# A hybrid attention and DeltaNet layer: one scan record per chunk, key and query chunks loaded by step, projections in another order

## Chip, core and metric

One core of a Trainium2 chip runs the whole program; it has one instruction stream for each engine (TensorE = PE, VectorE = DVE, ScalarE = ACT, GpSimd = POOL, SyncE = SP, which only issues DMAs). The metric is device time in microseconds (us), less is better.

## What is computed

Two layers; each normalises the tokens (256 context, 1024 sample), projects them once, runs latent attention and a two-way gated DeltaNet beside each other, gates both, projects them out and adds the residual.

```python
h = rmsnorm(x, norm_w) * (1.0 + scale) + shift
z = jnp.einsum('bsd,de->bse', h, w_in)
q_lat, kv_lat, k_pe, g_a, q_b, k_b, v_b, g_b, a_b, b_b = jnp.split(z, offs, axis=-1)
...
o_a = mla_attention(q_nope, q_pe, kv[..., :NOPE], kpe_all, kv[..., NOPE:]) * jax.nn.silu(g_a)
...
o_f, s_f = chunk_gated_delta(qc, kc, vc, g[:, :, 0], beta[:, :, 0], s0[:, 0])
o_r, s_r = chunk_gated_delta(flip(qc), flip(kc), flip(vc), flip(g[:, :, 1]), flip(beta[:, :, 1]), s0[:, 1])
...
out = jnp.einsum('bse,ed->bsd', jnp.concatenate([o_a, o_b], axis=-1), w_out)
x = x + gate * out
```

In the delta rule each chunk solves a triangular system, and a state of 128x128 is carried from chunk to chunk, once forward and once backward.

## The kernel before

The 1280 tokens are ten chunks of 128. The projection is 24 tiles of 128 columns (`misc`, `l0`, `l1`, `lk` of the latent attention, `k`, `q`, `v` of four DeltaNet heads, gates `ga`, `gb`); a tile is three products in split precision over eight blocks of the model dimension, `zp` in the trace. The string `ORDER` says in which order `w_thread` makes them. Their weights come by DMA (`wr`) and are split by DVE and POOL (`wh`, `wl`).

A DeltaNet head h goes through four pieces of code, each a Python generator ("thread"):

- `gram_thread` loads the head's keys and queries (`kq`) from the DRAM tensor `kqv_d`, in which the convolved projections lie, transposes the keys (`ktp`), makes for each chunk the products k·k and q·k (`gram`), scales them with decays (`dm`, `ai`) and writes them to DRAM, to `ai_d`. `kp_thread` makes on POOL the keys for the state update (`kpt`) and writes them to `kp_d`. `q_thread` takes the norm of the queries.
- `inv_thread` inverts the 32x32 diagonal blocks of all chunks at once: 31 pairs of DVE instructions (`wtmp`, then `W`), each waiting for the one before. Then, by `ph` and `px` on PE, the blocks are put together to the inverse of each chunk, which goes back into `ai_d`.
- `g_thread` is the scan: four chains (two directions, sample and context tokens), eight steps. A step loads its record `ti` (inverse and q·k) and `kp`, and is a line of dependent work: `ks` on PE (keys times state), `ru` on DVE, `up` on PE, a copy on ACT, `su` on PE, the state `S` on DVE, and `po` for the output. Keys and queries of the step are read from `kq`, which stays in SBUF as long as the scan runs. Since `kq` has two buffers, `gram_thread(h)` waits for the flag `scan{h-2}`.

The attention starts when all projections are done: `rope`, then for each of eight heads `prep` (`kp`, `qp` and the row maxima `pm`, each reduced by DVE, ending in one transposition `mxt`) and `main` (scores `sp`, exponentials on ACT, `po`). `main` of a head waits for its `prep`. After that comes the output projection, `wop`. DeltaNet heads that are not done run beside the attention.

The order of instructions on each engine is fixed when the program is built. Every engine call passes a helper (line 312) and is queued with its thread; a planner (`Sched.run`) takes again and again the call that can start first by its table of costs and latencies, with the thread's number in `PR` to break ties. Where the planner sees PE without work for too long it puts in filler matmuls whose result nobody reads (`spare`, line 433). Buffers of a pool are named by tag, with `bufs` copies each.

Of the kernel before, what the change touches and what calls it, by code (L numbers as in the profile page):

```python
# [16 lines left out]
P = 128  # L17
# [10 lines left out]
HB = 4  # L28
# [8 lines left out]
TAIL = 6  # L37
ORDER = 'misc k0 q0 v0 l0 l1 gb0 lk ga0 k1 q1 v1 k2 q2 v2 k3 q3 v3 gb1 gb2 gb3 ga1 ga2 ga3'
PR = dict(ada=2.2, w=2.5, e=2.4, load=2.3, s=1, g=2, p=2.1, kp=2.2, q2=2.2, lat=1, oa=2.45, rope=2.44, prep0=3, prep=3, vv=3, main=4, fin=2, ex=4, red=3, red0=3, prec=5, ldc=4.5, mm=5, fc=1)
# [355 lines left out]
def body(tc, I, O):  # L395
# [163 lines left out]
    def mixer(l, hhl):  # L559
# [6 lines left out]
        ap = bp = None  # L566
        kp_d = [dp.tile([NT, 2, P, P], F32, name=f"kp_d{l}_{h}") for h in range(HB)]
        ai_d = [dp.tile([2, NT, 2 * P * P + P], F32, name=f"ai_d{l}_{h}") for h in range(HB)]
        fl = lambda t: t.rearrange("p a b c -> p (a b c)")
# [305 lines left out]
        def w_thread():  # L875
            order = ORDER.split()
            need = {'q0': 'misc2', 'lk': 'latq', 'k1': 'latk'}
            steps = [(nm, (0, 1, 2)) for nm in order[:-TAIL]]
# [144 lines left out]
        def gram_thread(h):  # L1023
            if h:
                yield f"A{h-1}"
            if h >= 2:
                yield f"scan{h-2}"
            yield f"k{h}"
# [3 lines left out]
            be, gc, grow_d, kdx = (st_[q] for q in ("be", "gc", "grow_d", "kdx"))  # L1032
            kq = ap.tile([P, 2, TP], F32, tag="kq", name="kq", bufs=2)
            SY.dma_start(kq[:, 0, :], kqv_d[h][0])
# [26 lines left out]
            V.tensor_scalar(n2, k2, EPS, None, op0=ALU.add)  # L1061
            nn = ap.tile([P, NT], F32, tag="nn", name="nn", bufs=3)
            G.tensor_tensor(nn, n2, pw[:, 1:2].to_broadcast([P, NT]), op=ALU.pow)
# [3 lines left out]
            for d in range(2):  # L1067
                V.tensor_tensor(bp[:, d], be[:, d, :, h], n2, op=ALU.mult)
                V.tensor_tensor(kdb[:, d], kdx[:, d, :, h], bp[:, d], op=ALU.mult)
            hd[h] = dict(kq=kq, nn=nn)  # L1070
            sd.flag(f"nn{h}")
# [7 lines left out]
            for c in range(NT + 1):  # L1079
# [13 lines left out]
                if pend:  # L1093
                    x, px, pdm, pbk = pend
                    ai = ap.tile([P, 2, 2, P], F32, tag="ai", name="ai", bufs=2)
                    for d in range(2):
                        V.scalar_tensor_tensor(ai[:, d], in0=px, scalar=bp[:, d, x : x + 1], in1=pdm[d].unsqueeze(1).to_broadcast([P, 2, P]), op0=ALU.mult, op1=ALU.mult)
                    free(pbk)
                    SY.dma_start(ai_d[h][:, x, : 2 * P * P].rearrange("d (p a q) -> p d a q", p=P, a=2), ai)
                pend = (c, pt, dms, bk)  # L1100
# [3 lines left out]
        def inv_thread(h):  # L1104
# [24 lines left out]
            for d in range(2):  # L1129
                SY.dma_start(diag(wz, d), (WP if d else W)[64 * d : 64 * d + 40])  # L1130
                SY.dma_start(diag(ai_d[h], d), (W if d else WP)[64 * d : 64 * d + 40])
            for c0, m in groups:
                yield 0
# [39 lines left out]
        def kp_thread(h, ktok, kdb):  # L1173
            for c in range(NT):
                t = ap.tile([P, 2, P], F32, tag="kpt", name="kpt", bufs=2)
                for d in range(2):
                    G.tensor_scalar(t[:, d], ktok[:, c, :], kdb[:, d, c : c + 1], None, op0=ALU.mult)
                SY.dma_start(kp_d[h][c].rearrange("d p q -> p d q"), t)
                yield 0
            sd.flag(f"kp{h}")  # L1180

        def q_thread(h, kq):
            q2 = ap.tile([P, NT], F32, tag="q2", name="q2", bufs=3)
            for c0, m in groups:
# [13 lines left out]
        def g_thread(h):  # L1198
# [3 lines left out]
            yield f"nn{h}"  # L1202
            nn, kq = hd[h]["nn"], hd[h]["kq"]
            neg_eg, pos_eg, gle = (st_[q] for q in ("neg_eg", "pos_eg", "gle"))
            kch = lambda c: kq[:, 0, coff(c) : coff(c) + P]
            qch = lambda c: kq[:, 1, coff(c) : coff(c) + P]
            vt = ap.tile([P, TP], F32, tag="oT", name="vt", bufs=1)
# [29 lines left out]
            def load_rec(n):  # L1237
                for ci, d, c, samp, last in steps(n):
                    ti = ap.tile([P, 2, P], F32, tag="ti", name="ti", bufs=6)
                    SY.dma_start(ti, ai_d[h][d, c, : 2 * P * P].rearrange("(p a q) -> p a q", p=P, a=2))  # L1240
                    kp = None
                    if not (samp and last):
                        kp = ap.tile([P, P], F32, tag="kp", name="kp", bufs=6)
                        SY.dma_start(kp, kp_d[h][c, d])
                    rec[ci, n] = (ti, kp)

            load_rec(0)
            load_rec(1)
            for n in range(8):
# [6 lines left out]
                for ci, d, c, samp, last in act:  # L1256
                    if not (samp and last):
                        kps[ci] = rec[ci, n][1]
                    if state[ci] is not None:
                        p1s[ci] = yield from bank("ks")  # L1260
                        PE.matmul(p1s[ci][:, :P], kch(c), state[ci])
                yield 0
# [35 lines left out]
                for ci, d, c, samp, last in act:  # L1298
# [3 lines left out]
                    if old[ci] is not None:  # L1302
                        PE.matmul(po[:, 1, :], qch(c), old[ci])
                    pos[ci] = (po, bk)
# [509 lines left out]
        for h in range(HB):  # L1814
            sd.add(PR['p'], gram_thread(h))
            sd.add(PR['p'], inv_thread(h))
            sd.add(PR['g'], g_thread(h))
        sd.run()
# [87 lines left out]
```

## Time and profile before

| | |
|---|---|
| median of 3 runs | 2248.81 us (2247.12 to 2254.36) |
| the profiled execution | 2256.47 us |
| its span, first to last instruction | 2254.7 us |
| busy: PE, DVE, ACT, POOL | 2132.3, 1484.5, 772.3, 824.1 us |
| mean granted TensorE clock | 0.982 |
| DMA: moved, mean rate | 306.91 MB, 136 GB/s |

A busy time is the union of an engine's instructions. The granted clock is given as a share of full speed: 1.0 is 2.4 GHz, the lower level is 1.2 GHz, and a mean between them says how long each was granted. The DMA share is the mean busy share of the core's 16 DMA engines. A view of windows gives all of these for stretches counted in us from the span's start.

### The profile page before, as it was taken

The page shows a single profiled execution, that of the slowest core. Times are in us where ns is not written, and L with a number is a line of the kernel's source. Part 1 is how long each engine was busy: PE and PEld are TensorE (multiplying, and loading weights), DVE is VectorE, ACT ScalarE, POOL GpSimd, SP SyncE. Part 2 cuts the span into 40 slices and gives each one's busy share as a digit, 9 for nine tenths or more (in the row PEclk, how much of TensorE's full clock was granted, in tenths as well). Part 3 has the DMA queues.
Part 4 walks back from the last instruction along what each step waited for, and adds up shares of the span by engine and source line. Part 5 has one row for each costly group of instructions (what it writes and reads, how often), then busy time and mean ns, then how long its engine had stood idle before and what let it go on. Part 6 is the DMA issues. An engine that isn't in the chain of part 4 may idle for free. (4 is left out here: it accounts for less than half of the span.)

```text
span 2254.7 us, 35320 instructions
## 1 busy us (share of the span) xinstructions
PE 2132.3 (95%) x12292; PEld 1549.0 (69%) x12292; DVE 1484.5 (66%) x3085; ACT 772.3 (34%) x2120; POOL 824.1 (37%) x757
## 2 busy tenths in 40 slices
PE   8899999899989999999999999989998899999998
PEld 6667788787666665555777888878767566545576
DVE  4855468767787566564676667886767866665454
ACT  4243142322433345543122324342243334544311
POOL 2342132423442326644332423243333332665521
PEclk9999999999999999999999999999998899999999
DMA  7475674666743414102423555466765242320153
GB/s 271 124 234 160 200 238 136 187 197 202 225 115 85 119 42 126 42 18 75 129 100 91 160 155 174 148 201 199 229 189 144 51 129 64 103 60 19 40 159 108
DMA packets 365697, 306.91 MB, mean 136 GB/s; under 512 B 88480, under 2 KB 304000, under 8 KB 365264
## 3 DMA queue, kind: packets, MB, share of 16 engines
q1 hardware_dynamic: 365520, 304.66, 45.1%
q8 instruction: 98, 1.61, 0.3%
q14 instruction: 79, 0.65, 0.1%
HBM read 199.11 MB, written 105.46 MB: 135 GB/s over the span
## 5 line engine op out<-in xcount | busy, mean ns | idle before, releaser
L312 PE MATMUL zp<-hl,wh 128*128 128x512 f32 (+2 forms) x1128 | 419.9, 372 | 3.2 <-POOL hl L312 3.1
L312 PE MATMUL zp<-hh,wh 128*128 128x512 f32 (+2 forms) x1128 | 419.8, 372 | 2.5 <-ACT wd L312 0.8
L312 PE MATMUL zp<-hh,wl 128*128 128x512 f32 (+2 forms) x1128 | 419.0, 371 | 1.4 <-POOL wl L312 1.1
L312 POOL TENSOR_TENSOR wl<-wr,wh 128x512 fp32r<-128x512 f32 (+1 forms) x114 | 154.2, 1353 | 479.1 <-DVE wh L312 241.9
L312 ACT ACTIVATE pe<-sp 128x512 f32<-128x512 f32 (+1 forms) x352 | 201.3, 578 | 258.9 <-PE sp L312 243.6
L312 POOL TENSOR_TENSOR pe<-pe,pe 128x1024 f32<-128x1024 f32 x96 | 230.7, 2403 | 112.0 <-DVE pe L312 58.3
L312 DVE TENSOR_REDUCE at<-pm 128x1 f32<-128x512 f32 (+1 forms) x336 | 212.0, 682 | 71.4 <-PE pm L312 70.3
L312 PE MATMUL sp<-at 97*128 97x512 f32 (+1 forms) x704 | 239.1, 409 | 2.6 <-ACT pe L312 1.5
L312 PEld LDWEIGHTS zp<-hh,wh 128*128 128x128 f32 (+1 forms) x1128 | 214.4, 190 | 39.0 <-issue 5.3
L312 PEld LDWEIGHTS zp<-hl,wh 128*128 128x128 f32 (+1 forms) x1128 | 214.3, 190 | 38.3 <-issue 5.4
L312 PEld LDWEIGHTS zp<-hh,wl 128*128 128x128 f32 (+1 forms) x1128 | 214.4, 190 | 34.7 <-issue 4.1
L312 PE MATMUL po<-pe,vv 128*64 128x512 f32 (+1 forms) x768 | 189.2, 566 | 2.9 <-ACT pe L312 2.1
L312 PEld LDWEIGHTS sp<-at 97*128 97x128 f32 x704 | 122.3, 190 | 81.9 <-issue 46.7
L312 POOL TENSOR_SCALAR kpt<-ktok,kdb 128x128 f32<-128x128 f32 x160 | 107.0, 681 | 97.1 <-DMA kp_d<-kpt 68.7
L312 PE MATMUL pm<-at 96*128 96x512 f32 (+1 forms) x416 | 130.9, 389 | 8.4 <-DVE S L312 3.1
L312 PE MATMUL sp<-at,at 97*128 97x512 f32 (+1 forms) x352 | 137.4, 390 | 0.0
L312 DVE TENSOR_TENSOR pe<-pe,pe 128x256 f32<-128x256 f32 (+1 forms) x64 | 76.2, 1192 | 65.0 <-POOL pe L312 39.7
L312 PE MATMUL wop<-woh,ol 128*128 128x512 f32 x288 | 115.0, 399 | 3.5 <-POOL ol L312 3.5
L312 DVE TENSOR_TENSOR W<-W,wtmp 104x31 f32<-104x31 f32 (+15 forms) x248 | 114.6, 462 | 5.3
L312 PE MATMUL wop<-woh,oh 128*128 128x512 f32 x288 | 115.3, 400 | 1.6 <-DVE oh L312 1.6
L312 PEld LDWEIGHTS pm<-at 96*128 96x128 f32 x416 | 71.7, 192 | 63.2 <-ACT pe L312 17.9
L312 PE MATMUL wop<-wol,oh 128*128 128x512 f32 x288 | 115.0, 399 | 0.0
(267 smaller groups left out, 3926.3 us busy)
## 6 DMA issues: line engine op xcount, KB each, us to landing
wr<-in_w_main SPq DMA_DIRECT2D x116, 256.0 KB
ai_d<-ai SPq DMA_DIRECT2D x80, 256.0 KB
ti<-ai_d SPq DMA_DIRECT2D x160, 128.0 KB
wa<-in_w_ada SPq DMA_DIRECT2D x64, 256.0 KB
kqv_d<-yc SPq DMA_DIRECT2D x48, 256.5 KB
kq<-kqv_d SPq DMA_DIRECT2D x16, 641.0 KB
rb<-grow_d SPq DMA_DIRECT2D x80, 128.0 KB
kp_d<-kpt SPq DMA_DIRECT2D x80, 128.0 KB
```

Source lines behind the costliest of these rows:

```text
L312: op = Op(lambda: f(*a, **k), self.key, self.ns(name, a, k, aps), outs, [x for x in aps if x is not acc])
```

## The change

It has four parts. The record of a chunk and direction in DRAM holds three matrices (inverse, q·k and the keys for the state update), so `kp_d` is gone and a scan step loads one `ti` of three matrices. The scan no longer reads keys and queries from `kq`: each step loads its chunk of both from `kqv_d` into `kc`. With that `kq` needs one buffer, and `gram_thread(h)` waits for `q2{h-1}` (and, as before, `A{h-1}`) instead of `scan{h-2}`. The second half of `inv_thread` is a thread of its own, `t_thread`. And `ORDER` puts `k1 q1` ahead of `v0` and the latent tiles, `k2 q2` ahead of `v1`, `k3 q3` ahead of `v2`.

```diff
-ORDER = 'misc k0 q0 v0 l0 l1 gb0 lk ga0 k1 q1 v1 k2 q2 v2 k3 q3 v3 gb1 gb2 gb3 ga1 ga2 ga3'
+ORDER = 'misc k0 q0 k1 q1 v0 l0 l1 gb0 lk ga0 k2 q2 v1 k3 q3 v2 v3 gb1 gb2 gb3 ga1 ga2 ga3'
...
-        kp_d = [dp.tile([NT, 2, P, P], F32, name=f"kp_d{l}_{h}") for h in range(HB)]
-        ai_d = [dp.tile([2, NT, 2 * P * P + P], F32, name=f"ai_d{l}_{h}") for h in range(HB)]
+        ai_d = [dp.tile([2, NT, 3 * P * P + P], F32, name=f"ai_d{l}_{h}") for h in range(HB)]
+        rec3 = lambda t, x, a, b: t[:, x, : 3 * P * P].rearrange("d (p a q) -> p d a q", p=P, a=3)[:, :, a:b, :]
...
-            need = {'q0': 'misc2', 'lk': 'latq', 'k1': 'latk'}
+            need = {'q0': 'misc2', 'lk': 'latq', 'k2': 'latk'}
...
         def gram_thread(h):
             if h:
                 yield f"A{h-1}"
-            if h >= 2:
-                yield f"scan{h-2}"
+                yield f"q2{h-1}"
             yield f"k{h}"
...
-            kq = ap.tile([P, 2, TP], F32, tag="kq", name="kq", bufs=2)
+            kq = ap.tile([P, 2, TP], F32, tag="kq", name="kq", bufs=1)
...
-            nn = ap.tile([P, NT], F32, tag="nn", name="nn", bufs=3)
+            nn = ap.tile([P, NT], F32, tag="nn", name="nn", bufs=4)
...
-            hd[h] = dict(kq=kq, nn=nn)
+            hd[h] = dict(nn=nn)
...
-                    SY.dma_start(ai_d[h][:, x, : 2 * P * P].rearrange("d (p a q) -> p d a q", p=P, a=2), ai)
+                    SY.dma_start(rec3(ai_d[h], x, 0, 2), ai)
...
                 SY.dma_start(diag(ai_d[h], d), (W if d else WP)[64 * d : 64 * d + 40])
+            sd.flag(f"W{h}")
+
+        def t_thread(h):
+            if h:
+                yield f"T{h-1}"
+            yield f"W{h}"
+            wz = wz_d[h % 2]
             for c0, m in groups:
...
-                SY.dma_start(kp_d[h][c].rearrange("d p q -> p d q"), t)
+                SY.dma_start(rec3(ai_d[h], c, 2, 3), t.unsqueeze(2))
...
-            q2 = ap.tile([P, NT], F32, tag="q2", name="q2", bufs=3)
+            q2 = ap.tile([P, NT], F32, tag="q2", name="q2", bufs=4)
...
-                    ti = ap.tile([P, 2, P], F32, tag="ti", name="ti", bufs=6)
-                    SY.dma_start(ti, ai_d[h][d, c, : 2 * P * P].rearrange("(p a q) -> p a q", p=P, a=2))
-                    kp = None
-                    if not (samp and last):
-                        kp = ap.tile([P, P], F32, tag="kp", name="kp", bufs=6)
-                        SY.dma_start(kp, kp_d[h][c, d])
-                    rec[ci, n] = (ti, kp)
+                    ti = ap.tile([P, 3, P], F32, tag="ti", name="ti", bufs=6)
+                    m = 2 if samp and last else 3
+                    SY.dma_start(ti[:, :m], rec3(ai_d[h], c, 0, m)[:, d])
+                    kc = ap.tile([P, 2, P], F32, tag="kc", name="kc", bufs=6)
+                    SY.dma_start(kc, kqv_d[h][0:2, :, coff(c) : coff(c) + P].rearrange("j p q -> p j q"))
+                    rec[ci, n] = (ti, kc)
...
-                        kps[ci] = rec[ci, n][1]
+                        kps[ci] = rec[ci, n][0][:, 2, :]
...
-                        PE.matmul(p1s[ci][:, :P], kch(c), state[ci])
+                        PE.matmul(p1s[ci][:, :P], rec[ci, n][1][:, 0, :], state[ci])
...
-                        PE.matmul(po[:, 1, :], qch(c), old[ci])
+                        PE.matmul(po[:, 1, :], rec[ci, n][1][:, 1, :], old[ci])
...
             sd.add(PR['p'], inv_thread(h))
+            sd.add(PR['p'], t_thread(h))
             sd.add(PR['g'], g_thread(h))
```

The order of instructions moves with it. Three places:

DVE, first layer, the end of the first attention head's maxima. `at<-pm` are the reductions of the row maxima, `W<-W,wtmp` the steps of a block inversion, here head 3's. Before:

```order
L312 TENSOR_REDUCE at_5887<-pm 128x1 x4
L312 TENSOR_REDUCE at_5887<-pm 128x2
L312 TENSOR_REDUCE at_5887<-pm 128x1 x4
L312 TENSOR_REDUCE at_5887<-pm 128x2
L312 TENSOR_REDUCE at_5887<-at_5887 128x8
L312 SCALAR_TENSOR_TENSOR oT<-po,pos_eg,oT 128x128 x2
L312 SCALAR_TENSOR_TENSOR ru<-ks,neg_eg,vtok 128x128 x2
L312 TENSOR_TENSOR wtmp<-blk,W 104x31
L312 TENSOR_TENSOR W<-W,wtmp 104x31
L312 TENSOR_TENSOR wtmp<-blk,W 104x60
L312 TENSOR_TENSOR W<-W,wtmp 104x30x2
```

Now:

```order
L312 SCALAR_TENSOR_TENSOR thg<-thg,zp 128x512
L312 TENSOR_TENSOR W<-W,wtmp 104x2x30
L312 TENSOR_TENSOR wtmp<-blk,W 104x31
L312 TENSOR_TENSOR W<-W,wtmp 104x31
L312 TENSOR_TENSOR at_6487<-kp,at_6486 64x384
L312 SCALAR_TENSOR_TENSOR oT<-po,pos_eg,oT 128x128 x2
L312 TENSOR_TENSOR at_6487<-kp,at_6486 64x384 x3
L312 SCALAR_TENSOR_TENSOR ru<-ks,neg_eg,vtok 128x128 x2
L312 TENSOR_REDUCE at_6488<-pm 128x2
L312 SCALAR_TENSOR_TENSOR S_7166<-S_7038,gle,su 128x128
L312 SCALAR_TENSOR_TENSOR S_7167<-S_7039,gle,su 128x128
```

Before, head 3's inversion begins behind the last reduction of the first `prep`; now its last step stands ahead of the first reduction.

PE, first layer, around the transposition `mxt` that ends the first `prep`. `spare` is a filler, `x22` that it stands there 22 times. Before:

```order
L312 MATMUL pm<-at_5885 128x512 x4
L312 MATMUL pm<-at_5885 128x256 x2
L312 MATMUL ks<-S_7016,kq 128x128
L312 MATMUL ks<-S_7017,kq 128x128
L433 MATMUL spare<-ident 128x128 x22
L312 MATMUL mxt<-ident,at_5887 10x128
L433 MATMUL spare<-ident 128x128 x2
L312 MATMUL up<-ru,ti 128x128 x2
```

Now:

```order
L312 MATMUL pm<-at_6486 128x256
L312 MATMUL up<-ru,ti 128x128 x3
L312 MATMUL su<-ru,ti 128x128 x3
L433 MATMUL spare<-ident 128x128
L312 MATMUL mxt<-ident,at_6488 10x128
L312 MATMUL po<-ru,ti 128x128
L312 MATMUL po<-S_7382,kc 128x128
L312 MATMUL po<-ru,ti 128x128
```

Ahead of the transposition 22 fillers are now one, and two more behind it are gone. The scan steps around them (`ks` before, `up`, `su` now) are head 2's, the second step before, the fifth now. Counted over the whole order, the fillers behind the start-up are 147 before and 78 now: between the end of the projections and the second attention head's first `sp` in both layers 118 before and 50 now, later ones 29 and 8, and 20 in the first layer's projections, where none stood. All other PE instructions are the same in number and shape.

SP, first layer, the loads of the first scan steps of head 0. Before:

```order
L312 DMA ti<-ai_d_0_126 128x256
L312 DMA kp<-kp_d_0_122 128x128
L312 DMA ti<-ai_d_0_126 128x256
L312 DMA kp<-kp_d_0_122 128x128
L312 DMA ai_d_1_127<-ai 128x2x256
L312 DMA rb<-grow_d_1222 128x2x128
```

Now:

```order
L312 DMA wr<-in_w_main 128x512
L312 DMA ti<-ai_d_0_122 128x384
L312 DMA kc<-kqv_d_0_118 128x2x128
L312 DMA ti<-ai_d_0_122 128x384
L312 DMA kc<-kqv_d_0_118 128x2x128
L312 DMA ti<-ai_d_0_122 128x256
```

A chain's step has two loads as before: one record of 128x384 and one of key and query chunk, where the second was `kp`. Over the program SP issues 1610 DMAs, before 1594.

## Rows read from the trace of the kernel before

**Rows 1.** The page, parts 1 to 3: busy shares, digits of the granted clock, DMA queues.

```profile
PE 2132.3 (95%) x12292; PEld 1549.0 (69%) x12292; DVE 1484.5 (66%) x3085; ACT 772.3 (34%) x2120; POOL 824.1 (37%) x757
...
PEclk9999999999999999999999999999998899999999
...
q1 hardware_dynamic: 365520, 304.66, 45.1%
```

**Rows 2.** Windows: both projection phases (columns: busy us of each engine, granted clock, DMA share).

```profile
core 0: us, PE busy (x) PEld busy (x) DVE busy (x) ACT busy (x) POOL busy (x), PEclk, DMA share, GB/s
31.00:609.00 578.00, 545.30 (x3685) 424.61 (x3686) 386.42 (x933) 189.93 (x623) 182.70 (x228) 0.99 0.64 193
1179.00:1680.00 501.00, 481.58 (x2916) 399.91 (x2915) 356.44 (x858) 157.24 (x538) 167.24 (x206) 0.99 0.57 171
```

**Rows 3.** Windows: both transitions, from the last projection to the steady attention.

```profile
609.00:738.00 129.00, 115.07 (x700) 82.35 (x699) 101.29 (x223) 44.08 (x111) 41.77 (x40) 0.93 0.40 109
1680.00:1820.00 140.00, 118.46 (x711) 85.15 (x710) 108.94 (x235) 46.45 (x122) 43.84 (x42) 0.90 0.41 110
```

**Rows 4.** Windows of the filler matmuls alone, same two stretches.

```profile
609.00:738.00 129.00, 17.19 (x114) 16.23 (x114) 0.93 0.40 109
1680.00:1820.00 140.00, 17.55 (x122) 16.17 (x122) 0.90 0.41 110
```

**Rows 5.** Filler matmuls after the start-up, the view by tile from 500 us.

```profile
L433 PE MATMUL spare<-ident x294: 272/275/582, 629.3 to 2101.1; 128*128 128x128 f32 x147
```

**Rows 6.** Windows: steady attention of both layers.

```profile
870.00:1046.00 176.00, 173.51 (x783) 94.46 (x782) 102.39 (x135) 84.90 (x158) 109.55 (x64) 1.00 0.20 61
1940.00:2128.00 188.00, 183.97 (x824) 99.13 (x822) 107.59 (x141) 90.04 (x166) 114.71 (x68) 0.99 0.21 59
```

**Rows 7.** Groups of DVE by line, 651:738 (busy us, mean ns, idle before).

```profile
L312 DVE TENSOR_TENSOR W<-W,wtmp 104x156 f32<-104x156 f32 (+15 forms) x26 | 15.4, 594 | 0.7
L312 DVE TENSOR_REDUCE at<-pm 128x1 f32<-128x512 f32 (+1 forms) x21 | 13.6, 683 | 1.3 <-PE pm L312 1.3
L312 DVE TENSOR_TENSOR wtmp<-blk,W 104x156 f32<-104x156 f32 (+15 forms) x26 | 13.2, 506 | 0.4
```

**Rows 8.** By tile: head 2's ks, head 3's gram and head 3's W, first layer.

```profile
L312 PE MATMUL ks<-S,kq x36: 273/275/583, 628.6 to 718.9; 128*128 128x128 f32 x36
...
L312 PE MATMUL gram<-kq x20: 377/378/483, 583.5 to 619.5; 128*128 128x256 f32 x20
...
L312 DVE TENSOR_TENSOR W<-W,wtmp x31: 192/362/2473, 643.4 to 689.1; 104x31 f32<-104x31 f32 x2, 104x60 f32<-104x60 f32 x2, 104x87 f32<-104x87 f32 x2, 104x112 f32<-104x112 f32 x2
```

**Rows 9.** Windows: a projection stretch with crowded DMA, one with less.

```profile
1500.00:1520.00 20.00, 15.18 (x100) 11.71 (x99) 14.58 (x29) 5.12 (x13) 8.09 (x12) 1.00 0.94 278
1620.00:1650.00 30.00, 30.00 (x200) 23.82 (x200) 17.78 (x48) 6.89 (x29) 12.07 (x12) 1.00 0.72 222
```

**Rows 10.** The chain of waits, 1490:1545, its DMA pieces (start, us).

```profile
1499.87 5.31 DMA kp_d<-kpt
...
1505.20 5.13 DMA kqv_d<-yc
...
1532.71 2.60 DMA wr<-in_w_main
```

**Rows 11.** DMA issues by line with their sizes.

```profile
DMA packets 365697, 306.91 MB, mean 136 GB/s; under 512 B 88480, under 2 KB 304000, under 8 KB 365264
...
ai_d<-ai SPq DMA_DIRECT2D x80, 256.0 KB
ti<-ai_d SPq DMA_DIRECT2D x160, 128.0 KB
...
kq<-kqv_d SPq DMA_DIRECT2D x16, 641.0 KB
rb<-grow_d SPq DMA_DIRECT2D x80, 128.0 KB
kp_d<-kpt SPq DMA_DIRECT2D x80, 128.0 KB
...
kp<-kp_d SPq DMA_DIRECT2D x144, 64.0 KB
```

**Rows 12.** Issue time of a scan load on SP, by tile (ns min/median/max).

```profile
L312 SPq DMA_DIRECT2D ti<-ai_d x160: 319/382/1972, 280.5 to 1894.4; - x160
```

More of the change, by code (lines that the diff above doesn't have):

```diff
@@ L1202, in g_thread @@
             yield f"nn{h}"
-            nn, kq = hd[h]["nn"], hd[h]["kq"]
+            nn = hd[h]["nn"]
             neg_eg, pos_eg, gle = (st_[q] for q in ("neg_eg", "pos_eg", "gle"))
-            kch = lambda c: kq[:, 0, coff(c) : coff(c) + P]
-            qch = lambda c: kq[:, 1, coff(c) : coff(c) + P]
             vt = ap.tile([P, TP], F32, tag="oT", name="vt", bufs=1)
```

## The prediction

> **What bounds the kernel now.** I read the page's busy shares first. The reader should see that TensorE (PE) is busy for 2132 of 2255 us and no other engine for more than 66%, and that the granted clock is at full but for two slices late in the second layer [rows 1]. So PE time bounds the kernel, and a change can win only where PE is idle, works on fillers or runs at the lower clock level. The windows say where that is. In the two projection phases PE is busy 545.3 of 578 us and 481.6 of 501, with the clock at 0.99 [rows 2]. In the steady attention it is busy 173.5 of 176 us and 184.0 of 188, at full clock or nearly: nothing to win there [rows 6]. Between the two, in what I call the transitions (the last projection to the point where the second attention head has begun), PE is busy for only 115.1 of 129 us and 118.5 of 140, and the granted clock falls to 0.93 and 0.90 [rows 3]; of that busy time 17.2 and 17.6 us are fillers [rows 4]. What can be won in the transitions is therefore:
>
> - fillers, 17.2 + 17.6 = 34.8 us;
> - idle time, 13.9 + 21.5 = 35.4 us;
> - clock: a granted mean of 0.93 over 129 us lacks 0.07 x 129 = 9.0 us of full-speed time, 0.10 x 140 = 14.0 in the second layer, together 23.0 us. Part of this lies on idle or filler time and would be counted twice.
>
> Why PE waits there is seen on DVE: in the transitions it is busy for 101.3 of 129 and 108.9 of 140 us [rows 3], more densely than in the projections (386.4 of 578, 356.4 of 501 [rows 2]). In the groups of DVE the reader should see two users at once in 651:738: the attention's row maxima (21 instructions, 13.6 us) and the block inversion of DeltaNet head 3 (15.4 + 13.2 us of W and wtmp, each waiting for the last) [rows 7]. The view by tile says why they meet: head 3's gram runs from 583.5 to 619.5 and its inversion from 643.4 to 689.1 us, with head 2's scan from 628.6 to 718.9 beside them [rows 8], all because head 2's and head 3's gram had to wait for the scans of heads 0 and 1 to give back the key and query buffer.
>
> **The change part by part.** The sum is made against the profiled execution, 2256.5 us; the median of the runs shown is 7.7 us below it, 2248.8, and I give the result on that scale.
>
> *Earlier gram and inversion (the wait for the scan, the order of projections).* By the order, all of head 3's inversion now stands ahead of the first row-maximum reduction on DVE; so 28.6 us of DVE work in the first layer's transition [rows 7], and about as much in the second's, moves to the projection phase. There DVE has 578 - 386 = 192 and 501 - 356 = 145 us free [rows 2], which hides it; if that cover were gone, a serial chain of 28.6 us per layer would lie in front of the last projections' evacuation. The order counts what this does to PE: 147 fillers behind the start-up become 78, of which 20 are new ones in the first layer's projections. The price of a filler is 34.8 us / 118 = 0.30 us (a filler is two matmul records, so 114 and 122 records are 118 fillers [rows 4]; all behind the start-up are 294 records [rows 5]). So 69 x 0.30 = 20.7 us less. In the transitions alone they fall from 118 to 50, by 58%.
>
> Idle and low clock, 58.4 us, fall too, but not surely by as much: a filler marks a wait that the planner foresaw, and the scan step with its alternation of PE, DVE, PE, ACT, PE, DVE stays as long as it was. From both sides: nothing, since no row ties them to the fillers, and all 58.4. I take 40%, 23 us, nearer to the smaller half because the scan of head 2 still lies partly in the transition. What is late next there is the chain of the first attention head's own prep.
>
> *Work that moves is not work that goes.* Head 3's gram and part of head 2's scan take the same PE time in the projection phase as behind it: zero in the sum, whichever side the projection's end moves to.
>
> *Key and query chunks by step.* 160 loads of 128 KB are added, 21.0 MB, and 144 loads of 64 KB disappear into the larger record, whose bytes are the same [rows 11]. SP issues 16 more DMAs at 0.38 us [rows 12], 6 us of a queue that is not on PE's path: zero, and if the queue were late, 6 us. In DMA time the page has 45.1% of 2254.7 us for 304.66 MB [rows 1], 3.34 us per MB, so 70 us of all 16 engines, 35 us per layer, of which three heads in four, 26 us, in the projection phase. Head 3's gram brings along 10 x (256 + 128 + 128) KB and two loads of 641 KB [rows 11], 6.6 MB or 22 us, and the larger part of head 2's scan loads (20 x 128 KB and 18 x 64 KB, 3.8 MB) another 13. Together 61 us per layer: the DMA share of the projection phases rises from 0.64 and 0.57 [rows 2] to about (370 + 61)/598 = 0.72 and (286 + 61)/521 = 0.67 if they get 20 us longer. A stretch at 0.72 kept PE busy for all of its 30 us; one at 0.94 lost 4.8 of 20 [rows 9]. On the mean nothing is lost, then, but bursts reach the upper value. I charge one more crowded stretch of 20 us per layer, 2 x 4.8 = 10 us; the bounds are 0 and six stretches, 29 us. What such a stretch does is in the chain of waits: in it kp_d and kqv_d land after 5.31 and 5.13 us, a weight load 25 us later after 2.60 [rows 10], so the cost is 2.7 us for each landing that somebody waits for. The Trainium skill (DMA: Bandwidth & Descriptors, section on latency and other measured facts) gives an HBM access latency of 0.2 us on average and 2 us at high load; by that, an estimate of 1.8 us per landing, the charge would be some 7 us instead of 10 and the sum 3 us lower. The trace agrees on the direction, with the larger number.
>
> *One buffer for kq, the wait for q2.* The load of the next head's kq now waits on SP for the last gram matmul of the head before, and weight loads are queued behind it. The planner sets the thread free only behind that head's gram, so the wait is short; the nearest row is the longest issue of a scan load, 1.97 us [rows 12]. Six such waits (three heads, two layers) are 12 us at most; I take zero, since weights have two buffers. The thread cut in two adds no instruction: zero. The larger record: zero.
>
> Sum: -20.7 - 23 + 10 = -34 us; 2256.5 - 34 = 2222.5 as a profiled execution, **2215** beside the median.
>
> **Rivals.**
>
> *Crowded DMA eats it (slower).* The transfers that move go where DMA is busiest, the last third of each projection phase, some 21 stretches of 20 us from 400 to 609 and 1460 to 1680. If 14 of them behaved like the one at 0.94, the loss would be 14 x 4.8 = 67 us against 44 won (20.7 + 23): +23 us, 2272. It decides from 44 / 4.8, about nine stretches on. For it: the row at 0.94 exists already [rows 9, 10]. Against it: the mean stays near 0.7, and the gram of heads 1 to 3 is spread over more of the phase.
>
> *The gaps only move (no change).* PE then waits in the projections as long as it waited in the transitions: the 20 new fillers are the sign of it, and scan steps placed among projections wait for evacuation on a DVE that has more to do. If the 44 us won come back but for 5, the time is 2244. That the change doesn't do what it says is part of this rival: if the gram of head 3 still runs late because its projections k3 and q3 stand only two tiles ahead of v3, the last of the heads, the inversion meets the maxima again.
>
> *All of it is won (much faster).* With the DVE freed, fillers fall as counted and idle and clock go to full: -20.7 - 58.4 = -79 us, 2170. Against it: the scan's own alternation leaves idle time in any stretch in which it has no projection beside it.
>
> **How the numbers follow.** A measurement of this kernel can tell about 0.3%, 6.7 us, from no change. Forecast: 0.58, with its own range from 2190 (two thirds of idle and clock, no crowding) to 2240 (fillers only, 10 us crowding, rounded up). Everything won: 0.12. Gaps only move: 0.13. Crowded DMA: 0.17. Faster is the first two, 0.70; same 0.13; slower 0.17. The range from 2182 to 2262 leaves out the lower half of the second case and somewhat over half of the last, about 0.16 in all.
>
> **What would show it.** Right: fillers behind the start-up fall to 156 records; head 3's W ends before the first pm; idle time in the transitions falls by a third or more, with a granted clock above 0.95 there; PE's busy share in the projection phases stays at 0.94 or above. The DMA step is wrong if several stretches of the projection phases show a share over 0.9 with PE under 16 of 20 us. The whole is wrong if the projection phases grow by more than the transitions shrink, or if PE in the transitions waits as long without DVE beside it, for then the scan's latency and not DVE held it.

## The result and the profile after

The changed kernel takes 2222.47 us (median of 4 runs, 2217.9 to 2228.78), the kernel before 2251.43 (4 runs on the same chip). The ratio is 0.9875, 95% interval 0.9843 to 0.9906: 28 us less. The profiled execution took 2217.9 us, the shortest of the four, with a span of 2216.1; against the 2254.7 of before that is 38.6 us less, so the stages below overstate the gain by some 10 us.

The page of the changed kernel, parts 1 to 3 (before: [rows 1]):

```profile
PE 2097.0 (95%) x12154; PEld 1519.9 (69%) x12154; DVE 1442.9 (65%) x3085; ACT 771.0 (35%) x2120; POOL 847.4 (38%) x757
...
PEclk9999999989999999999999999999999999999999
...
q1 hardware_dynamic: 388304, 325.63, 48.9%
```

PE is busy 35.3 us less: 20.8 of that are fillers (below), 14.5 other matmuls that took less time. Its idle time, span less busy time, hardly falls: 122.4 to 119.1 us. DMA moved the 21 MB more that were counted.

Windows of the changed kernel, both layers: projections, transition, attention (columns as in [rows 2]; before: [rows 2, 3]):

```profile
30.00:624.00 594.00, 554.44 (x3779) 435.46 (x3779) 409.69 (x1012) 194.01 (x630) 204.62 (x244) 0.98 0.68 207
624.00:740.00 116.00, 107.45 (x719) 76.27 (x717) 79.29 (x179) 44.26 (x118) 34.78 (x26) 0.99 0.52 148
740.00:1035.00 295.00, 285.93 (x1340) 158.90 (x1340) 173.24 (x264) 138.58 (x282) 155.65 (x92) 0.99 0.20 59
1164.00:1676.00 512.00, 487.40 (x2964) 404.07 (x2962) 366.58 (x922) 162.35 (x559) 189.84 (x225) 1.00 0.65 191
1676.00:1795.00 119.00, 110.91 (x712) 78.30 (x712) 87.97 (x206) 43.76 (x118) 33.34 (x26) 0.96 0.52 146
1795.00:2093.00 298.00, 287.52 (x1336) 159.01 (x1336) 174.28 (x261) 138.02 (x282) 155.49 (x92) 0.98 0.20 58
```

Cut at the same events (first and last `zp` of each layer, first `sp` of the second attention head, first `wop`), the stages compare so, in us, by the windows shown:

| stage | before | after | PE idle before | after |
|---|---|---|---|---|
| projections | 578 + 501 | 594 + 512 | 32.7 + 19.4 | 39.6 + 24.6 |
| transitions | 129 + 140 | 116 + 119 | 13.9 + 21.5 | 8.6 + 8.1 |
| attention | 309 + 309 | 295 + 298 | 6.1 + 7.5 | 9.1 + 10.5 |
| output | 132 + 126 | 129 + 123 | 6.5 + 10.4 | 6.2 + 8.6 |

The projections grow by some 26 us, the transitions shrink by 34, the attention by 25. Part of this is moved work: in the projections PE has 94 and some 45 instructions more, and in the attention, where the scans of the last heads used to end, 166 and 134 fewer. The idle time moves as well: 19 us less in the transitions, 12 more in the projections, 6 more in the attention.

Windows of the filler matmuls alone in the changed kernel, the transitions and the whole span (before: [rows 4]):

```profile
624.00:740.00 116.00, 7.38 (x54) 6.58 (x54) 0.99 0.52 148
1676.00:1795.00 119.00, 5.95 (x46) 5.61 (x46) 0.96 0.52 146
...
0.00:2216.00 2216.00, 54.28 (x362) 48.29 (x362) 0.99 0.49 148
```

Over the whole span they were 75.1 us before, so 20.8 less. Behind the start-up there are 156 records of them (before: [rows 5]), by tile:

```profile
L433 PE MATMUL spare<-ident x156: 272/275/583, 487.7 to 2064.7; 128*128 128x128 f32 x156
```

Head 3's inversion in the first layer of the changed kernel, by tile (before: [rows 8]):

```profile
L312 DVE TENSOR_TENSOR W<-W,wtmp x31: 191/376/1376, 592.7 to 628.4; 104x31 f32<-104x31 f32 x2, 104x60 f32<-104x60 f32 x2, 104x87 f32<-104x87 f32 x2, 104x112 f32<-104x112 f32 x2
```

It ends 4 us behind the last projection (628 against 624) and ahead of the first row maximum, which DVE reduces at 633.2; before it began 34 us behind the last projection (643 against 609). In the second layer it is not as early:

```profile
L312 DVE TENSOR_TENSOR W<-W,wtmp x31: 178/378/1019, 1658.4 to 1699.4; 104x31 f32<-104x31 f32 x2, 104x60 f32<-104x60 f32 x2, 104x87 f32<-104x87 f32 x2, 104x112 f32<-104x112 f32 x2
```

There it still runs 23 us past the last projection (1676) and 10 us past the first row maximum (1689.3). DVE in the transitions is busy for 79 of 116 and 88 of 119 us instead of 101 of 129 and 109 of 140.

Where the projections now lose time is seen in four stretches of the changed kernel (before: [rows 9]):

```profile
460.00:480.00 20.00, 13.74 (x82) 11.14 (x80) 19.86 (x52) 8.07 (x36) 18.66 (x16) 0.91 0.48 150
1500.00:1520.00 20.00, 19.51 (x129) 16.22 (x128) 10.98 (x22) 7.18 (x19) 5.13 (x10) 1.00 0.92 271
1520.00:1540.00 20.00, 16.11 (x97) 14.46 (x95) 19.76 (x54) 9.24 (x43) 13.93 (x9) 0.91 0.53 155
1580.00:1600.00 20.00, 19.31 (x155) 17.38 (x154) 13.90 (x40) 4.97 (x15) 2.96 (x4) 1.00 1.01 310
```

At a DMA share of 0.92 and 1.01 PE loses under 1 us of 20; the worst stretch of 20 us at 0.9 or more, 220 to 240, lost 1.6. PE loses 4 to 6 where DVE (third engine) is full for 19.8 of 20 us, at a share of 0.5. The waits of PE, whole program, show the same (us in total, times, longest):

```profile
PE pd L312 <- DVE pe L312: 11.0, 3, 5.5
PE up L312 <- DVE ru L312: 10.4, 14, 2.6
PE adap L312 <- DMA wa<-in_w_ada: 7.1, 8, 2.4
PE zp L312 <- DVE ai L312: 6.9, 1, 6.9
...
PE ph L312 <- DMA tt<-ai_d: 3.9, 2, 2.9
```

The longest single wait, 6.9 us at 475 to 482, is a projection held up behind DVE's work on `ai`, the inversion's input that now comes among the projections.

### The profile page after: what moved, and what is told of

Same layout as the page of the kernel before. It is cut to its first block, busy times and chain, and to the rows that moved or that the text cites. A ratio compares the mean times of both kernels' runs of the same rounds, so it can differ in the third digit from the quotient of the medians.

```text
span 2216.1 us, 35036 instructions
## 1 busy us (share of the span) xinstructions
PE 2097.0 (95%) x12154; PEld 1519.9 (69%) x12154; DVE 1442.9 (65%) x3085; ACT 771.0 (35%) x2120; POOL 847.4 (38%) x757
## 3 DMA queue, kind: packets, MB, share of 16 engines
q1 hardware_dynamic: 388304, 325.63, 48.9%
## 5 line engine op out<-in xcount | busy, mean ns | idle before, releaser
L312 POOL TENSOR_SCALAR kpt<-ktok,kdb 128x128 f32<-128x128 f32 x160 | 130.0, 824 | 94.1 <-DMA ai_d<-kpt 84.4
L312 PEld LDWEIGHTS pm<-at 96*128 96x128 f32 x416 | 70.9, 191 | 61.5 <-ACT pe L312 21.4
L312 DVE TENSOR_TENSOR wtmp<-blk,W 104x31 f32<-104x31 f32 (+15 forms) x248 | 105.6, 426 | 4.6 <-POOL W L312 0.9
```

Source lines behind the costliest of these rows:

```text
L312: op = Op(lambda: f(*a, **k), self.key, self.ns(name, a, k, aps), outs, [x for x in aps if x is not acc])
```

## Experiments

Theory: the gain is that of the prediction, the wait for the scan gone and DVE free in the transitions; the loads by step cost about 10 us. Rivals: another order alone brings it; each change of the program makes the planner write another plan, and the plan of before was an unlucky one; the fillers cost nothing, and count waits only. Ratios are to the kernel before on the same chip, with 95% intervals. The change was timed once, ahead of the runs; runs 1 to 4, 5 to 8 and 9 to 12 were timed on three chips, on which the kernel before had medians of 2252.9, 2253.8 and 2258.5 us. A difference between a run and the change therefore goes by way of the kernel before, and its interval is that of both.

**1. The order of the projections alone**, in the kernel before.

```diff
-ORDER = 'misc k0 q0 v0 l0 l1 gb0 lk ga0 k1 q1 v1 k2 q2 v2 k3 q3 v3 gb1 gb2 gb3 ga1 ga2 ga3'
+ORDER = 'misc k0 q0 k1 q1 v0 l0 l1 gb0 lk ga0 k2 q2 v1 k3 q3 v2 v3 gb1 gb2 gb3 ga1 ga2 ga3'
...
-            need = {'q0': 'misc2', 'lk': 'latq', 'k1': 'latk'}
+            need = {'q0': 'misc2', 'lk': 'latq', 'k2': 'latk'}
```

> The kernel before with the new order of projections alone; the wait for the scan, two key and query buffers, separate records stay. Its order has 114 fillers behind the start-up (before 147, the change 78). Theory A (the gain is that gram and inversion of heads 2 and 3 no longer wait for a scan): the wait is still there, so at most the fillers' difference is won, 33 x 0.30 = 10 us: about 2240. Rival B (the order of the projections gives the gain by itself): 2222, as the whole change.

Measured: 0.9927 (0.9901 to 0.9953), more than half of the gain. In its trace head 3's inversion of the first layer runs from 572.8 to 616 us, ahead of the first row maximum (621.0), though the wait for the scan is in place: there the order of the projections alone moves it.

**2. The change with the old order** (both lines above as they were before).

> The changed kernel with the old order of projections; the wait for the scan is gone. Its order has 224 fillers behind the start-up. Theory A: gram no longer waits, but k3 and q3 come as late as before, so half of the gain, about 2235. Rival B: 2250. By the filler count alone: (224 - 78) x 0.30 = 44 us above the change, 2266.

Measured: 1.0124 (1.0091 to 1.0157), slower than either kernel. The two halves by themselves give -0.7% and +1.2%, the whole -1.25%: they don't add. With the wait gone, the inversion runs from 624.1 to 675 us, again among the row maxima (from 628.2 on).

**3. The change with the wait for the scan back.**

```diff
                 yield f"A{h-1}"
                 yield f"q2{h-1}"
+            if h >= 2:
+                yield f"scan{h-2}"
```

> The changed kernel with one line more: gram of head h waits for the scan of head h-2 again, all else as changed. Its order has 150 fillers. Theory A: nearly all of the gain is lost, 2245 to 2250, and head 3's inversion meets the row maxima again. Rival B: 2222 to 2228. A third theory, C (the single record and the loads by step give the gain): 2222 as well.

Measured: 0.9917 (0.9889 to 0.9944). Two thirds of the gain stay with the wait in place, and with nearly as much filler time as before: 70.9 us over the span against 75.1. As expected of theory A, the inversion meets the row maxima again (591.9 to 643 us, the first maximum at 612.5), yet most of the gain is there. The removed wait is not what most of the gain hangs on: it is worth 0.0042, 9 us, give or take 9.

**4. The change with `kp_d` apart again**, planned anew.

```diff
-                SY.dma_start(rec3(ai_d[h], c, 2, 3), t.unsqueeze(2))
+                SY.dma_start(kp_d[h][c].rearrange("d p q -> p d q"), t)
...
-                    m = 2 if samp and last else 3
-                    SY.dma_start(ti[:, :m], rec3(ai_d[h], c, 0, m)[:, d])
+                    SY.dma_start(ti[:, :2], ai_d[h][d, c, : 2 * P * P].rearrange("(p a q) -> p a q", p=P, a=2))
+                    if not (samp and last):
+                        SY.dma_start(ti[:, 2], kp_d[h][c, d])
```

> The changed kernel with the keys for the state update in a record of their own again (separate tensor in DRAM, 144 more loads of 64 KB, 320 scan loads become 464). Its order has 137 fillers. Theory A: the record has no part in the gain, 2222 plus at most the price of the fillers, 59 x 0.30 = 18 us: 2222 to 2240. Theory C: 2245 or more, and the added wait is on SP's queue or on a DMA landing.

Measured: 1.0005 (0.9989 to 1.0022); the whole gain is gone. Either 144 more loads cost 29 us (0.013 x 2251), or the new plan does. Run 5 tells these apart. Head 3's inversion in its first layer:

```profile
L312 DVE TENSOR_TENSOR W<-W,wtmp x31: 185/374/1356, 566.8 to 609.8; 104x31 f32<-104x31 f32 x2, 104x60 f32<-104x60 f32 x2, 104x87 f32<-104x87 f32 x2, 104x112 f32<-104x112 f32 x2
```

The projections end at 622 here, the first row maximum comes at 633.8: the inversion is as early as after the change, and the kernel is no faster than before.

**5. The same two loads, with the order of all instructions held to that of the change**: the planner counts one load, two are issued (`Call` hands the planner's one call to a function of ours; the keys are written to `kp_d` in the same way).

```diff
-                    SY.dma_start(ti[:, :m], rec3(ai_d[h], c, 0, m)[:, d])
+                    def two(ti=ti, m=m, c=c, d=d):
+                        nc.sync.dma_start(ti[:, :2], rec3(ai_d[h], c, 0, 2)[:, d])
+                        if m == 3:
+                            nc.sync.dma_start(ti[:, 2], kp_d[h][c, d])
+                    Eng(Call(two), "D").dma_start(ti[:, :m], rec3(ai_d[h], c, 0, m)[:, d])
```

> The changed kernel with its order of instructions held fixed on every engine, but with the state-update keys in a tensor of their own: 144 more loads of 64 KB are issued on SP behind the record loads, without the planner knowing. The run with two records lost the whole gain (ratio 1.0005). Theory C (the single record itself saves the time, on SP's queue or in the DMA engines): the same loss here, 2245 or more. Theory P (the loss came from the other order that the planner then made; the loads themselves are hidden): 2222 to 2230, at most 144 x 0.38 us of SP's queue showing in part.

Measured: 0.9926 (0.9893 to 0.9959), 0.0051 above the change, which is 11 us, give or take 10 by the two intervals. So some 18 of run 4's 29 us were its plan, and the one record is worth about 11, at the same bytes. That the loads themselves, and not their 62 us of issue time on SP (144 x 0.43 us), cost the 11 is not shown.

**6. Each key and query chunk loaded twice**, the second time into a buffer that nobody reads, the order again that of the change: 160 more loads, 21 MB.

```diff
                     SY.dma_start(kc, kqv_d[h][0:2, :, coff(c) : coff(c) + P].rearrange("j p q -> p j q"))
+                    k2 = ap.tile([P, 2, P], F32, tag="kc2", name="kc2", bufs=4)
+                    Sched.push(lambda k2=k2, c=c: nc.sync.dma_start(k2, kqv_d[h][0:2, :, coff(c) : coff(c) + P].rearrange("j p q -> p j q")))
```

> The changed kernel with its order held fixed and every key and query chunk loaded a second time into a buffer that nobody reads: 160 more loads of 128 KB, 21 MB, by my estimate 70 us of all 16 DMA engines, most of it in the projection phases. If crowded DMA costs PE time (the term of 10 us in the prediction, and its slower rival): 10 us or more longer, 2232 to 2245. If DMA has room, as the stretches at a share of 0.92 and 1.01 with PE at 19.5 and 19.3 of 20 us in the changed kernel suggest: 2222 to 2228.

Measured: 0.9999 (0.9976 to 1.0022), 0.0124 above the change: 28 us, give or take 9. By doubling, this is the price of the loads by step. SP issues the added loads in 0.47 us each, 75 us in all, and the run doesn't tell this time on SP's queue from the traffic:

```profile
L1249 SPq DMA_DIRECT2D kc<-kqv_d x160: 359/467/1364, 291.8 to 1858.8; - x160
```

The windows of this run, both projection phases (its profiled execution was among the longest of ten, that of the change the shortest of four, so 40 us lie between the two traces):

```profile
30.00:633.00 603.00, 559.62 (x3781) 439.70 (x3782) 408.56 (x1010) 194.64 (x631) 203.65 (x244) 0.97 0.71 213
1181.00:1711.00 530.00, 493.81 (x2962) 407.91 (x2959) 367.99 (x921) 163.21 (x560) 188.38 (x225) 0.98 0.66 196
```

They are 9 and 18 us longer than after the change, with the same instructions; idle time there rises from 64 to 80 us, and the granted clock falls from 0.98 and 1.00 to 0.97 and 0.98. The mean DMA share has hardly moved, 0.68 and 0.65 to 0.71 and 0.66, because the stretch got longer with it. PE waits 30 times for a landing, 36.9 us in all, where after the change it was 20 times and 20.2 us. Three of the waits that have grown:

```profile
PE adap L312 <- DMA wa<-in_w_ada: 9.7, 10, 2.6
...
PE ph L312 <- DMA tt<-ai_d: 7.6, 4, 2.9
...
PE ks L312 <- DMA kc<-kqv_d: 3.7, 4, 1.5
```

For `ph` it was 3.9, for `adap` 7.1. The waits are more, but the longest of most is little changed; that for `kc` grows from 0.4 to 1.5 us, and a new one for `ti` takes 3.2.

**7 to 10. Other plans of both programs.** One constant of the planner's table is changed by 1.5 or 2%; the program computes and loads the same, only the order differs. Run 7 is the change and run 8 the kernel before, with the cost of a DMA byte changed; 9 and 10 the same two, with DVE's fixed cost changed.

```diff
-            return m * (160 if b < 16 else 8 + b / 26 + (9 if b < 512 else 0)) / 16
+            return m * (160 if b < 16 else 8 + b / 25.5 + (9 if b < 512 else 0)) / 16
...
-        return 67 + n * (0.53 if fast else 6.3 if name == "reciprocal" else 1.045) + 61 * ptr
+        return 68 + n * (0.53 if fast else 6.3 if name == "reciprocal" else 1.045) + 61 * ptr
```

Run 7:

> The changed kernel with one constant of the planner's table changed by 2% (the cost of a DMA's bytes), no instruction added, removed or altered: only the order differs, with 86 fillers behind the start-up instead of 78. Theory P (any change of the program makes another plan, and plans differ by up to one per cent): between 2205 and 2250, anywhere. If the planner's result is steady and the parts of the change have worths of their own: 2222 plus 8 x 0.30 = 2 us, within 5 us of the change.

Run 8:

> The kernel before with the same constant changed by 2%: only the order differs, with 123 fillers behind the start-up instead of 147. Theory P: between 2230 and 2275, anywhere. Steady plans: 2251 less 24 x 0.30 = 7 us, 2244, within 5 us.

Run 9:

> The changed kernel with another constant of the planner's table nudged (the fixed cost of a DVE instruction 68 for 67 ns); only the order differs, 80 fillers behind the start-up. A third plan of the same program: its two others stand at 0.9875 and 0.9901 of the kernel before. If the change has a worth of its own beyond the plan, it falls near them: 0.983 to 0.995.

Run 10:

> The kernel before with the same nudge; only the order differs, 121 fillers. Its two other plans stand at 1 and 0.9906. If the plan the change was compared with was an unlucky one, this falls at 0.985 to 0.995 and the change's own worth is some 0.3% or nothing; if the first nudge was a lucky one, at 0.997 to 1.005.

| plan | kernel before | the change |
|---|---|---|
| as written | 1 | 0.9875 (0.9843 to 0.9906) |
| DMA byte | 0.9906 (0.9874 to 0.9937) | 0.9901 (0.987 to 0.9933) |
| DVE fixed cost | 0.9869 (0.9851 to 0.9887) | 0.9884 (0.985 to 0.9918) |

All five other plans lie within 0.4% of each other; only the kernel before as written stands apart. A 2% edit of a planner's constant, or one of 1.5%, brings to the kernel before about as much as the whole change. That the edited constants simply make better plans is unlikely, for they bring the change nothing. Windows of run 10, its transitions, and its head 3's inversion by tile:

```profile
603.00:719.00 116.00, 105.49 (x647) 74.83 (x646) 95.44 (x216) 43.31 (x110) 41.35 (x41) 0.94 0.44 119
1663.00:1783.00 120.00, 106.89 (x636) 73.27 (x634) 101.48 (x234) 45.32 (x118) 42.09 (x41) 0.94 0.42 118
```

```profile
L312 DVE TENSOR_TENSOR W<-W,wtmp x31: 178/360/2382, 632.5 to 674.9; 104x31 f32<-104x31 f32 x2, 104x60 f32<-104x60 f32 x2, 104x87 f32<-104x87 f32 x2, 104x112 f32<-104x112 f32 x2
```

Here the inversion still lies behind the projections (which end at 603), among the row maxima, and DVE is as dense as before (0.82 and 0.85 of the stretch, [rows 3] 0.79 and 0.78). The transitions are as short as after the change, 116 and 120 us. But the same length holds less work here. Fillers in them:

```profile
603.00:719.00 116.00, 10.95 (x70) 10.19 (x70) 0.94 0.44 119
1663.00:1783.00 120.00, 12.25 (x82) 11.29 (x82) 0.94 0.42 118
```

PE's busy time without fillers is 189 us in the two, 205 after the change, 199 before. Idle time and fillers together are 70 us before, 47 in run 10 and 30 after the change: more than half of the fall comes with the meeting in place, the rest does not. In run 8 too the inversion runs late, from 633.4 to 680 us, behind projections that end at 604.

**11. The new order and the one record**, with keys and queries kept in `kq` and the wait for the scan: the two parts that runs 1 and 5 had found to pay, without the loads (the new `ORDER` and the new record's writes, as in the change, are left out here).

```diff
-                    ti = ap.tile([P, 2, P], F32, tag="ti", name="ti", bufs=6)
-                    SY.dma_start(ti, ai_d[h][d, c, : 2 * P * P].rearrange("(p a q) -> p a q", p=P, a=2))
-                    kp = None
-                    if not (samp and last):
-                        kp = ap.tile([P, P], F32, tag="kp", name="kp", bufs=6)
-                        SY.dma_start(kp, kp_d[h][c, d])
+                    ti = ap.tile([P, 3, P], F32, tag="ti", name="ti", bufs=6)
+                    m = 2 if samp and last else 3
+                    SY.dma_start(ti[:, :m], rec3(ai_d[h], c, 0, m)[:, d])
+                    kp = ti[:, 2, :]
```

> The kernel before with the new order of projections and the single record, but keys and queries kept in SBUF: no loads by step, 21 MB less than in the change, the wait for the scan stays; 180 fillers. By prices at a fixed order (the second loading of the chunks cost 28 us, the split record 11) and with the wait worth 9 (the run that put it back): 2222 - 28 + 9 = 2203. By the fillers: 102 x 0.30 = 31 us above the change, 2253. If the plan decides more than the parts: anywhere from 2205 to 2255.

Measured: 0.9916 (0.9893 to 0.9938), 2239.94 us against 2258.49. The sum of the prices, which gave 2203, missed by some 30 us (0.9916 x 2251 is 2232); the count of fillers, which gave 2253, missed too: with 78.6 us of fillers over the span, more than the kernel before, it is faster by 0.8%.

**12. The change without fillers behind the start-up**, in the same order.

```diff
-        for _ in range(n):
+        for _ in range(n if Sched.seq < 900 else 0):
             Sched.spin()
```

> The changed kernel, the same order, with all fillers behind the start-up left out (22.7 us of filler time in its trace, 78 fillers). If a filler costs the time it takes, 2222 - 20 = 2202. If it only fills a wait that is there anyway, and keeps the clock up: the same or slower, 2222 to 2240, idle time up by about 20 us and the granted clock lower behind the gaps.

Measured: 0.986 (0.9838 to 0.9882), no different from the change's 0.9875: 3 us less, give or take 8, where the price of a filler asked for 20. The page of this run, and its transitions:

```profile
PE 2098.2 (94%) x11998; PEld 1513.5 (68%) x11998; DVE 1446.4 (65%) x3085; ACT 772.1 (35%) x2120; POOL 848.0 (38%) x757
```

```profile
626.00:748.00 122.00, 106.53 (x663) 73.42 (x660) 79.12 (x178) 44.08 (x118) 34.68 (x26) 0.92 0.51 144
1689.00:1808.00 119.00, 108.30 (x669) 75.31 (x669) 88.11 (x207) 44.20 (x118) 33.29 (x25) 0.94 0.53 147
```

The 156 records, 22.7 us, are gone, yet PE is busy for as long (2097.0 to 2098.2), because the mean granted clock falls from 0.986 to 0.977 (0.99 and 0.96 to 0.92 and 0.94 in the transitions) and the real matmuls take that much more. Idle time rises from 119.1 to 132.3 us. The four runs had clocks of 0.977 to 0.979, those of the change 0.982 to 0.986. Taking 22.7 us of fillers away won nothing that can be measured: what they stand for is a wait, which stays.

The split of `inv_thread` by itself was not run: put back into one thread, the order of instructions on every engine is the same, so it changes nothing here.

## Why the prediction was right, and where it was not

**The number.** 2215 forecast, 2222.47 measured, inside the range and in the likeliest case. Most signs that the prediction named came: 156 filler records; head 3's inversion ahead of the maxima, in the first layer alone; 53% less idle time in the transitions (35.4 to 16.6 us) at a clock of 0.99 and 0.96; projections that grow by some 26 us while the transitions shrink by 34. PE's busy share in the projections is 0.933 and 0.952, where 0.94 or above was asked. That the sum came out is in good part luck, as the parts show: its largest terms came with another plan, for which the mechanism given is not shown to be the cause, and two smaller ones missed and partly cancelled.

**"Earlier gram and inversion", the fillers (-20.7 us).** Filler time fell by 20.8 us, as counted. As a price this step failed: run 12 shows that fillers taken away by themselves win nothing, and runs 3 and 11 are faster than before with 70.9 and 78.6 us of them. The term was right by what it went along with, not by what it is.

**The same step, idle and low clock (-23 us).** In the transitions it was too careful: -19 us idle, and of clock 5.9 us are lacking (0.01 x 116 + 0.04 x 119) instead of 23.0. Over the program it was too high: 18 us of idle came back in projections and attention, and the total fell by 3. The rival "the gaps only move" was right for the idle time. For the clock the runs don't decide: its mean is 0.982 in the one trace and 0.986 in the other, 41 us lacking and 31, but over all its runs the kernel before shows 0.976 to 0.988.

**The cause given for both, DVE's meeting of inversion and maxima.** This is the part that failed. In the changed kernel the meeting is gone in the first layer; in the second it is cut to 10 us, though the prediction had all of the inversion ahead of the maxima. Its reason, "all because head 2's and head 3's gram had to wait for the scans", is not what the runs show for the first layer: run 1 keeps the wait and has no meeting, run 2 drops the wait and has it. And the time of the whole does not go with the meeting: it is gone in run 4's first layer and so is the gain; it is there in runs 3, 8 and 10, and most or all of the gain too. A part of the shorter transitions may still be its due (30 us of idle time and fillers against run 10's 47), but no run holds all else fixed.

What the runs point to is that the plan of the kernel before was an unlucky one: two others of the same program are 0.9 and 1.3% faster. What in that plan costs the time stays open. The mean of three plans is 0.9925 for the kernel before and 0.9887 for the change, and without the plan as written 0.9888 for the kernel before. By these means the change is worth between nothing and 0.4% beyond a new plan; three plans of each do not settle it.

**"Key and query chunks by step" (+10 us).** The price by doubling is 28 us, close to the upper bound of 29, and not by crowded stretches as charged: no stretch of 20 us at a share of 0.9 or more lost PE over 1.6 us after the change, where the one charged had lost 4.8. Landings are waited for more often in run 6 (30 waits against 20), idle time in the projections goes from 64 to 80 us, and the clock falls with it. The charge went by stretches of a high mean share and could not see this. Its 2.7 us per landing was moreover the difference between two writes to DRAM (5.31 and 5.13 us) and a read of weights (2.60), which are not alike. The Trainium skill (DMA: Bandwidth & Descriptors, section on latency and other measured facts) has the access latency of HBM rise with load, and by it the charge would have been 7 us. Both figures lie below the price by doubling, but no run here shows that latency by itself, and the longest of most waits did not grow.

**"The larger record: zero."** About 11 us won (run 5), though with an interval of 10. Loads and record together are some 17 us by these prices, 10 in the sum: two misses that partly cancel. Run 11 shows that such prices can't be added to predict another plan.

**"Work that moves", one buffer for kq, the thread cut in two.** Nothing speaks against zero: after the change SP waits once, 0.5 us, for a gram matmul, and PE once, 1.9 us, for `kq`. The moved work shows in the instruction counts of the stages.

No run is clearly faster than the change: 10 (0.9869) and 12 (0.986) equal it within their intervals.

## What to carry to other kernels

Where a planner writes the order, move one of its constants by a per cent or two and time that first, for the kernel before as well: if the time moves as much as the change does, one plan of each says nothing of the cause. To price a load or an instruction, hold the order fixed and add or double it. Fillers, idle time and low clock in a stretch are three faces of one wait, so count them once, and ask what the wait becomes in the next stage.

## What was not expected of the hardware

160 loads of 128 KB whose data nobody reads cost 28 us (give or take 9), their issue on SP included, at a mean DMA share of 0.49 over the program, as much as the change wins. 144 more loads at the same bytes (325.63 and 325.64 MB on the hardware queue) cost about 11, give or take 10. In 20 us at a DMA share of 1.01 PE lost 0.7. And fillers just paid for themselves: 22.7 us of them against 20 us of full-speed time (0.986 to 0.977 of some 2220 us) and no measurable change in the time.
